# Eight kept weights' splits moved into the first part's down projection, half stores, and the tail as one written order

## The chip, the cores and the metric

One core of a Trainium2 chip runs the whole program. The metric is device time in microseconds of one launch; lower is better. Of the kernel before there are three timed runs and one profiled execution.

## The reference

One step of a two-layer backbone over 640 tokens (512 latent, 128 context) of width 1024. Layer 0 mixes by attention, layer 1 by a gated linear recurrence (LRU); each is followed by a gated feed-forward network of inner width 2816, and at the end stands one RMS norm. What matters for the change:

```python
def _swiglu(x, w_gu, w_down):
    gate, up = jnp.split(x @ w_gu, 2, axis=-1)
    return (jax.nn.silu(gate) * up) @ w_down

def _rms_norm(x, g):
    xf = x.astype(jnp.float32)
    y = xf * lax.rsqrt(jnp.mean(xf * xf, axis=-1, keepdims=True) + RMS_EPS)
    return (y * g.astype(jnp.float32)).astype(x.dtype)
...
    # each sub-layer: pre-norm, scale and shift from silu(cond) @ w_mod + b_mod, gated residual add
    y_prompt = _rms_norm(ctx, final_g)
    y_sample = _rms_norm(lat, final_g)
```

## The kernel before

Activations lie with the 1024 features on partitions in 8 tiles (`x[:, f, tokens]`), tokens along the free axis. Every product of fp32 data is made of three passes of matmuls: each operand is split into a rounded high half and the rest as low half, and `chunk` (L233) adds high x high (L240), high x low (L241) and low x high (L242) for each of the feature tiles into one PSUM tile (`mm` or `mx`). The split is a cast on ScalarE (ACT) and a subtraction on VectorE (DVE), `split`, L1443 and L1444. A weight that is used once is loaded through SyncE's queue as `raw` and split into `whi`/`wlo` or `whx`/`wlx` by `unit` (L174).

**Feed-forward of layer 0** (`ffn`, L838 to 878). The 22 inner tiles are done in three parts of 8, 7 and 7. In a part's gate and up stage, each inner tile j takes one gate and one up product; DVE multiplies with the norm's `r` and adds (`sg`, `up`), ACT applies SiLU, and the hidden tile is split into halves in `big`. Then the part's down projection follows: `project` (L567) runs over 8 output tiles f, each with a product over the part's tiles and a residual add to `x` (L562). The third part's down projection is also the entry to the next layer. In the trace: part one's gate and up stage 394 to 500 us, its down projection 500 to 556; part two 556 to 655 and 655 to 705; part three 705 to 805 and 805 to 860.

**Kept splits** (`keep`, L199 to 210, called in L872). 29 weights of the later layer, the recurrence's input and output products (16 `wi`, 8 `wlo`) and five tiles of the next feed-forward (`gu`), are split ahead of time, while PE is busy with layer 0's feed-forward, and the halves are put into DRAM; `unit` later loads both halves with no work on ACT and DVE. A keep is: load 512 KB into `mraw` (three buffers, shared with the modulations) through POOL's queue, cast on ACT (L207) and subtract on DVE (L208) into the two halves of one buffer `kw`, one store of 1 MB through POOL's queue (L210). It is issued behind the split of the last hidden tile (`self.mark`). Before, two are called in each step j of parts two and three, and three in the last step of each.

**Modulations** (`fill`, `mod_cols`, L271 to 281). The adaLN columns of later sub-layers are worked out in the background: a load of 512 KB into `mraw` through POOL's queue, and two DVE products with accumulation (`mprod`, L279), one for each of the two conditioning vectors. `done` and `ws` call `fill`.

**The tail** (`project_last`, L596 to 645). The last down projection is done in two token ranges, first 384 tokens for all 8 output tiles, then 256. In the second, each product p0 to p7 is followed by a residual add; ACT squares the sums, POOL adds squares up (L627). The final norm's statistics of a range: `root` (L483) takes the second moment by matmuls with ones (`at`, L488), then mean and root (`var`, a power on POOL or a square root with a correction step on ACT and DVE), `diag` (L504) puts the result on a diagonal (`dg`, L505), and `spread` (L507) brings it to all partitions by matmuls with ones (L509). Then DVE multiplies `x` by the column of `final_g` and the spread value (L613 for the first range, 8 of 384 columns; L640 for the second, 8 of 256), and SyncE stores pairs of tiles.

**What sets the order.** ACT, DVE, PE and POOL each run their instructions in program order. That order is set by a scheduler that interleaves the written steps, `issue_after` gives it edges, and a block under `in_order` keeps the order in which it is written.

Of the kernel before, what the change touches and what calls it, by code (L numbers as in the profile page):

```python
# [9 lines left out]
F32 = mybir.dt.float32  # L10
F32R = mybir.dt.float32r
AF = mybir.ActivationFunctionType
ALU = mybir.AluOpType
AX = mybir.AxisListType

P = 128
D = 1024
KT = D // P
# [17 lines left out]
ORDERED = (mybir.EngineType.PE, mybir.EngineType.DVE, mybir.EngineType.Activation)  # L36
C0 = 515
FG = (1, 1, 1)
MODS = ((0, 2), (0, 4), (0, 3), (0, 5), (1, 1), (1, 0), (1, 4), (1, 3), (1, 2), (1, 5))
NB = 2  # L40
KH = KT // 2
HT = NTOK // 2
# [11 lines left out]

COLS = ["ng00", "ng01", "ng10", "ng11", "cw0", "cw1", "cw2", "cw3", "cb",
        "ba0", "ba1", "bi0", "bi1", "lam0", "lam1", "h0", "h1", "bsh", "bsc", "fg"] + [f"bm{l}{j}" for l, j in MODS]
# [77 lines left out]
class _Step:  # L134
# [64 lines left out]
    def keep(self, todo, n):  # L199
        nc = self.nc  # L200
        for _ in range(min(n, len(todo))):
            name, f = key = todo.pop(0)
            raw = self.t([P, D], F32, "mraw", 3, self.sb).rearrange("p (k m) -> p k m", k=KT)
            nc.gpsimd.dma_start(raw, self.i[name][1, f] if name == "gu" else self.i[name][f])
            w = self.t([P, 2, KT, P], F32R, "kw", 1, self.sb)
            with self.tc.issue_after(self.mark[0]), self.tc.issue_after(self.mark[1]):
                nc.scalar.copy(w[:, 0], raw)  # L207
                nc.vector.tensor_tensor(w[:, 1], raw, w[:, 0].bitcast(F32), ALU.subtract)  # L208
            self.kept[key] = d = self.dram.tile([P, 2 * D], F32, tag=f"k{name}{f}", name=f"k{name}{f}")
            nc.gpsimd.dma_start(d, w.rearrange("p h k m -> p (h k m)").bitcast(F32))  # L210

    def two(self, src, x):
        nc = self.nc
# [257 lines left out]
    def square(self, k, t0, t1):  # L471
        nc = self.nc
        s = slice(t0, t1)
        if k == 0:
            nc.scalar.activation(self.ssq[:, s], self.x[:, k, s], AF.Square)
            return
        q = self.t([P, 384], F32, "sq", 2, self.sb)[:, :t1 - t0]
        self.sqr = nc.scalar.activation(q, self.x[:, k, s], AF.Square).ins
        if k < KT - 1 or self.whole:
            nc.vector.tensor_tensor(self.ssq[:, s], self.ssq[:, s], q, ALU.add)  # L480
        self.lastq[t0] = [q]
# [22 lines left out]
    def diag(self, dg, r, n):  # L504
        self.dg = self.nc.vector.tensor_tensor(dg, self.ident.unsqueeze(1).broadcast_to([P, n, P]), r.unsqueeze(2).broadcast_to([P, n, P]), ALU.mult).ins  # L505
# [90 lines left out]
    def project_last(self, w, hi, lo, gk):  # L596
        nc, tc = self.nc, self.tc
        G = self.need(self.gcols, gk)
        us = []
        for f in range(0, KT, 2):  # L600
            us += self.two(w[f:f + 2], f % 4)
        (a0, a1), (b0, b1) = CHL
        self.ssq = self.t([P, NTOK], F32, "ssq", 1, self.sb)
        for f, u in enumerate(us):
            self.residual(f, a0, a1, self.chunk(u, hi, lo, a0, a1), G, True)
        with tc.issue_after(self.sqr):
            nc.scalar.activation(self.t([P, 1], F32, "dum", 1), self.ones[:, 0:1], AF.Sqrt)
        mm = self.stat(a0, a1)
        r0 = self.r[0][:, 0:a1 - a0]

        def final(k):
            xs = self.x[:, k, a0:a1]
            nc.vector.scalar_tensor_tensor(xs, xs, self.col("fg", k), r0, ALU.mult, ALU.mult)  # L613

        def store(k, t0, t1):
            nc.sync.dma_start(self.o["y"][k * P - P:k * P + P, t0:t1].rearrange("(k p) t -> p k t", p=P), self.x[:, k - 1:k + 1, t0:t1])

        squares = []
        for f, u in enumerate(us):
            with tc.issue_after(mm) if f == KT - 1 else nullcontext():  # L620
                ps = self.chunk(u, hi, lo, b0, b1)
            last = self.residual(f, b0, b1, ps, G, False)
            xs = self.x[:, f, b0:b1]
            q = self.ssq[:, b0:b1] if f == 0 else self.t([P, HT], F32, "snap", 3, self.sb)[:, 0:b1 - b0]
            nc.scalar.activation(q, xs, AF.Square)
            if 0 < f < KT - 3:
                nc.gpsimd.tensor_tensor(self.ssq[:, b0:b1], self.ssq[:, b0:b1], q, ALU.add)  # L627
            squares.append(q)
            if f > 1:
                with tc.issue_after(last):  # L630
                    final(f - 2)
        self.lastq[b0] = squares[KT - 3:]
        self.stat(b0, b1, True)
        r1 = self.r[0][:, 0:b1 - b0]
        with tc.issue_after(self.dg):
            for k in range(KT - 2, KT):
                final(k)
        for k in range(KT):
            xs = self.x[:, k, b0:b1]
            nc.vector.scalar_tensor_tensor(xs, xs, self.col("fg", k), r1, ALU.mult, ALU.mult)  # L640
        for k in (1, 3):
            store(k, a0, a1)
        for t0, t1, ks in ((b0, b1, (1,)), (a0, a1, (5, 7)), (b0, b1, (3, 5, 7))):
            for k in ks:
                store(k, t0, t1)


    def qk(self, p, hi, lo, ap, acc=None):
        nc = self.nc
# [188 lines left out]
    def ffn(self, l, hi, lo, fp, last):  # L838
        nc = self.nc
        f0 = 0  # L840
        todo = [("wi", KT), ("wi", 0)] + [("wi", f + g) for f in range(1, KT) for g in (KT, 0)] + [("wlo", f) for f in range(KT)]
        todo += [("gu", c * NF + f) for f in range(PLAIN) for c in range(2)] + [("gu", PLAIN)]
        for ci, n in enumerate((8, 7, 7)):
            hhi = self.big()
            hlo = self.big()
            sg = {}

            def eg(j):
                def ev(t0, s, ps):
                    if t0:  # L850
                        sg[j] = self.t([P, NTOK], F32, "sg", 2, fp)
                    g = sg[j]
                    nc.vector.tensor_tensor(g[:, s], ps, self.rt[:, s], ALU.mult)
                    for c, a, b in _pieces(s.start, s.stop):
                        nc.scalar.activation(g[:, a:b], g[:, a:b], AF.Silu, bias=self.bias[:, c:c + 1])
                return ev

            def eu(j):
                def ev(t0, s, ps):
                    u = self.t([P, 320], F32, "up", 2, fp)  # L860
                    nc.vector.tensor_tensor(u, ps, self.rt[:, s], ALU.mult)
                    for c, a, b in _pieces(s.start, s.stop):
                        g = sg[j][:, a:b]
                        nc.vector.scalar_tensor_tensor(g, u[:, a - t0:b - t0], self.bias[:, c:c + 1], g, ALU.add, ALU.mult)
                    self.mark = self.split(hhi[:, j, s], hlo[:, j, s], sg[j][:, s])
                return ev
            for j in range(n):
                f = f0 + j
                self.ws(self.i["gu"][l, f], hi, lo, eg(j), FG[0] * (f > 0), CHB)
                self.ws(self.i["gu"][l, NF + f], hi, lo, eu(j), FG[1] * (f > 0), CHB)  # L870
                if ci:
                    self.keep(todo, 3 if j == n - 1 else 2)  # L872
            w = self.i["dn"][l, :, :, f0:f0 + n]
            if ci == 2:
                last(w, hhi, hlo, (l, 5))
            else:
                self.project(w, hhi, hlo, (l, 5), done=lambda f: self.fill(FG[2]))
            f0 += n


# [707 lines left out]
```

## Time and profile before

| | |
|---|---|
| median of 3 runs | 1515.62 us (1513.51 to 1517.41) |
| profiled execution, device time | 1514.37 us |
| its span | 1512.6 us |
| mean granted TensorE clock | 0.993 |
| PE / DVE / ACT / POOL busy | 98% / 71% / 47% / 17% |
| DMA, mean over the span | 163 GB/s |
| DMA, 556 to 655 us | 283 GB/s, 0.84 of the engines' time |

The profile's rows give busy time for each engine. A row of waits names the engine and line that waited, what released it, the total, the number of times and the longest. The chain of waits goes back from an end to what released each step, so a DMA in it is one that something stood still for. Rows of windows give busy time of each engine in a stretch, then the granted clock, the share of time that the 16 DMA engines were busy, and GB/s.

### The profile page before, as it was taken

What the parts mean: (1) busy time and instruction counts of PE and PEld (TensorE: products, weight loads), DVE (VectorE), ACT (ScalarE), POOL (GpSimd) and SP (SyncE); (2) the same over time, 40 slices, a digit from 0 to 9 for tenths busy, and PEclk for the clock granted to TensorE, in tenths of its full rate; (3) what the DMA queues carried; (4) which work ended last, traced back from release to release, by engine and by line L of the source; (5) the groups of instructions that cost most, each with busy time, mean ns of one, the idle gap of its engine ahead of it and who ended that gap; (6) DMA issues with size and microseconds to landing.
All of it is one profiled execution on the core that took longest, in us unless ns stands there. A gap on an engine that the chain in (4) does not pass through costs nothing.

```text
span 1512.6 us, 26116 instructions
## 1 busy us (share of the span) xinstructions
PE 1477.8 (98%) x10303; PEld 1432.5 (95%) x10303; DVE 1078.4 (71%) x2044; ACT 716.5 (47%) x1320; POOL 256.4 (17%) x315
## 2 busy tenths in 40 slices
PE   7999999999999999999999999999999999999997
PEld 4999999889999999999999988899999999999996
DVE  5788887869996337869787468885875675665646
ACT  5676766654333124322435378863644343424342
POOL 0212221100110001111111001122123323232211
PEclk9999999999999999999999999999999999999999
DMA  9554554445563228987898733246333131313111
GB/s 374 168 161 144 181 166 140 117 154 182 168 199 120 74 94 289 313 295 264 305 310 309 267 124 128 71 160 229 118 130 89 57 112 56 112 57 107 62 57 70
DMA packets 79530, 246.99 MB, mean 163 GB/s; under 512 B 8832, under 2 KB 22320, under 8 KB 75568
## 3 DMA queue, kind: packets, MB, share of 16 engines
q1 hardware_dynamic: 58416, 154.97, 31.3%
q0 software_dynamic: 20672, 90.20, 18.0%
q8 instruction: 81, 1.33, 0.4%
q14 instruction: 41, 0.34, 0.1%
q10 hardware_dynamic: 320, 0.16, 0.0%
HBM read 202.02 MB, written 39.34 MB: 160 GB/s over the span
## 4 chain that ended last, share of the span: by engine, by line
PE 79%; DMA 8%; DVE 6%; ACT 3%; issue 3%; POOL 1%; SPq 0%; POOLq 0%; DVEq 0%; ACTq 0%
PE mm L240 12%; PE mm L241 12%; PE mm L242 12%; PE mx L240 4%; PE mx L242 4%; PE mx L241 4%; PE mx L1132 3%; PE mx L1133 3%; PE mx L1134 3%; PE gp L1338 2%; DMA mraw<-in_wm 2%; PE op L826 2%; PE tp L743 2%; DMA kwi<-kw 1%; DMA kwlo<-kw 1%
## 5 line engine op out<-in xcount | busy, mean ns | idle before, releaser
L241 PE MATMUL mm<-big,whi 128*128 128x320 f32 (+2 forms) x1003 | 312.2, 311 | 4.0 <-DVE big L1444 4.0
L240 PE MATMUL mm<-big,whi 128*128 128x320 f32 (+2 forms) x1003 | 311.1, 313 | 1.8 <-ACT big L1443 1.0
L242 PE MATMUL mm<-big,wlo 128*128 128x320 f32 (+2 forms) x1003 | 311.8, 312 | 0.0
L279 DVE SCALAR_TENSOR_TENSOR mprod<-mraw,csb 128x1024 f32<-128x1024 f32 x160 | 195.9, 1225 | 9.3 <-DMA mraw<-in_wm 9.1
L241 PEld LDWEIGHTS mm<-big,whi 128*128 128x128 f32 x1003 | 189.8, 189 | 6.1 <-DVE big L1444 5.0
L240 PEld LDWEIGHTS mm<-big,whi 128*128 128x128 f32 x1003 | 189.2, 189 | 4.7 <-ACT big L1443 1.9
L242 PEld LDWEIGHTS mm<-big,wlo 128*128 128x128 f32 x1003 | 189.7, 189 | 1.1
L1443 ACT CAST whi<-raw 128x1024 fp32r<-128x1024 f32 (+2 forms) x103 | 105.7, 1027 | 150.3 <-PE mm L241 96.5
L1444 DVE TENSOR_TENSOR wlo<-raw,whi 128x1024 fp32r<-128x1024 f32 (+2 forms) x103 | 127.0, 1233 | 36.3 <-ACT whi L1443 36.0
L241 PE MATMUL mm<-big,whx 128*128 128x320 f32 (+3 forms) x450 | 140.0, 311 | 0.0
L242 PE MATMUL mm<-big,wlx 128*128 128x320 f32 (+3 forms) x450 | 140.0, 311 | 0.0
L240 PE MATMUL mm<-big,whx 128*128 128x320 f32 (+3 forms) x450 | 139.9, 311 | 0.0
L562 DVE SCALAR_TENSOR_TENSOR x<-mm,G,x 128x320 f32<-128x320 f32 (+3 forms) x207 | 83.5, 437 | 78.3 <-PE mm L242 70.4
L240 PE MATMUL mx<-big,whi 128*128 128x320 f32 (+2 forms) x325 | 101.7, 313 | 0.2 <-ACT whi L1443 0.2
L242 PE MATMUL mx<-big,wlo 128*128 128x320 f32 (+2 forms) x325 | 100.8, 310 | 0.0
L241 PE MATMUL mx<-big,whi 128*128 128x320 f32 (+2 forms) x325 | 100.6, 310 | 0.0
L275 POOL DMA_DIRECT2D mraw<-in_wm x80 | 43.2, 540 | 325.6 <-DVE mprod L279 211.3
L241 PEld LDWEIGHTS mm<-big,whx 128*128 128x128 f32 x450 | 85.6, 190 | 0.0
L240 PEld LDWEIGHTS mm<-big,whx 128*128 128x128 f32 x450 | 85.6, 190 | 0.0
L242 PEld LDWEIGHTS mm<-big,wlx 128*128 128x128 f32 x450 | 85.6, 190 | 0.0
L240 PE MATMUL mx<-big,whx 128*128 128x320 f32 (+3 forms) x222 | 69.1, 311 | 0.0
L242 PE MATMUL mx<-big,wlx 128*128 128x320 f32 (+3 forms) x222 | 69.0, 311 | 0.0
(370 smaller groups left out, 3813.3 us busy)
## 6 DMA issues: line engine op xcount, KB each, us to landing
raw<-in_gu SPq DMA_DIRECT2D x84, 512.0 KB, 3.6
mraw<-in_wm POOLq DMA_DIRECT2D x80, 512.0 KB, 4.3
kwi<-kw POOLq DMA_DIRECT2D x16, 1024.0 KB, 5.3
raw<-in_dn SPq DMA_DIRECT2D x24, 512.0 KB, 3.6
raw<-in_wqk SPq DMA_DIRECT2D x16, 512.0 KB, 4.0
sw<-in_wm SPq DMA_DIRECT2D x16, 512.0 KB, 10.2
mraw<-in_wi POOLq DMA_DIRECT2D x16, 512.0 KB, 5.2
kwlo<-kw POOLq DMA_DIRECT2D x8, 1024.0 KB, 5.2
```

The lines of the kernel that those rows point to most:

```text
L240: nc.tensor.matmul(ps, hi[:, k], xhi[:, k, s], start=(k == 0), stop=False)
L241: nc.tensor.matmul(ps, hi[:, k], xlo[:, k, s], start=False, stop=False)
L242: nc.tensor.matmul(ps, lo[:, k], xhi[:, k, s], start=False, stop=(k == nk - 1))
L275: nc.gpsimd.dma_start(w, self.i["wm"][l * 6 + j - 2, f])
L279: nc.vector.scalar_tensor_tensor(prod, w, 1.0, self.csb[:, s], ALU.mult, ALU.mult, accum_out=out[:, s, f:f + 1])
L562: last = self.nc.vector.scalar_tensor_tensor(xs, ps[:, a - t0:b - t0], G[:, s, f:f + 1], xs, ALU.mult, ALU.add).ins
L743: nc.tensor.transpose(tp[:, j * P:j * P + P], s[:, j * P:j * P + P], self.ident)
L1132: nc.tensor.matmul(ps, hi[:, k], xh[:, k], start=start and k == 0, stop=False, skip_group_check=not start)
L1133: nc.tensor.matmul(ps, hi[:, k], xl[:, k], start=False, stop=False, skip_group_check=not start)
L1134: nc.tensor.matmul(ps, lo[:, k], xh[:, k], start=False, stop=(k == KH - 1), skip_group_check=not start)
L1443: high = self.nc.scalar.copy(hi, v).ins
L1444: return high, self.nc.vector.tensor_tensor(lo, v, hi.bitcast(F32), ALU.subtract).ins
```

## The change

**Kept splits.** The buffer `kw` becomes two, `kwh` and `kwl`, and the 1 MB store two of 512 KB, both issued behind the subtraction in the program. Part one's down projection calls one keep behind each of its 8 output tiles. Part two calls two in each of the first six steps, part three in each of the first seven; 9 are left for it, so they go to steps 0 to 4. No keep is called at a part's last step.

**The tail.** Its steps stand in one written order (`TAIL`), kept on PE, DVE, ACT and POOL. The multiplication with `final_g` moves to ACT, on `x` itself (16 new activations with a column as scale: `gain`, 8 of 384 columns and 8 of 256), placed ahead of the finals. The finals become products with the spread value alone: four of two tiles with 384 columns, two of four tiles with 256, each with its store. POOL adds five squares instead of four, so the second moment is taken of three parts instead of four. The first range's moment (`m`) stands after p1 and its spread (`x`) after p3. Three matmuls with ones stand ahead of the last spread; nothing reads their result, which the spread overwrites.

```diff
+LATE = (0, 6, 7)
...
+TAIL = (
+    "p0 T r0 p1 m r1 q0 q1 t1 p2 d r2 q2 t2 p3 x r3 s0 s1 q3 t3 p4 F0 r4 F2 s2 q4 t4 p5 r5 F4 s3 q5 t5 p6 r6 s4 F6 q6 s5 s6 p7 r7 q7 s7 y67 ")
...
         for _ in range(min(n, len(todo))):
             name, f = key = todo.pop(0)
-            raw = self.t([P, D], F32, "mraw", 3, self.sb).rearrange("p (k m) -> p k m", k=KT)
-            nc.gpsimd.dma_start(raw, self.i[name][1, f] if name == "gu" else self.i[name][f])
-            w = self.t([P, 2, KT, P], F32R, "kw", 1, self.sb)
+            raw = self.t([P, D], F32, "mraw", 3, self.sb)
+            nc.gpsimd.dma_start(raw.rearrange("p (k m) -> p k m", k=KT), self.i[name][1, f] if name == "gu" else self.i[name][f])
+            self.kept[key] = d = self.dram.tile([P, 2 * D], F32, tag=f"k{name}{f}", name=f"k{name}{f}")
+            high, low = [self.t([P, D], F32R, n, 1, self.sb) for n in ("kwh", "kwl")]
             with self.tc.issue_after(self.mark[0]), self.tc.issue_after(self.mark[1]):
-                nc.scalar.copy(w[:, 0], raw)
-                nc.vector.tensor_tensor(w[:, 1], raw, w[:, 0].bitcast(F32), ALU.subtract)
-            self.kept[key] = d = self.dram.tile([P, 2 * D], F32, tag=f"k{name}{f}", name=f"k{name}{f}")
-            nc.gpsimd.dma_start(d, w.rearrange("p h k m -> p (h k m)").bitcast(F32))
+                nc.scalar.copy(high, raw)
+                nc.vector.tensor_tensor(low, raw, high.bitcast(F32), ALU.subtract)
+            for h, w in enumerate((high, low)):
+                nc.gpsimd.dma_start(d[:, h * D:h * D + D], w.bitcast(F32))
...
+        def gain(f, t0, t1):
+            nc.scalar.activation(x[:, f, t0:t1], x[:, f, t0:t1], AF.Copy, scale=self.col("fg", f))
...
-            nc.vector.scalar_tensor_tensor(xs, xs, self.col("fg", k), r0, ALU.mult, ALU.mult)
...
-        for k in range(KT):
-            xs = self.x[:, k, b0:b1]
-            nc.vector.scalar_tensor_tensor(xs, xs, self.col("fg", k), r1, ALU.mult, ALU.mult)
...
+        def final(k0, k1, t0, t1, r):
+            v = x[:, k0:k1, t0:t1]
+            nc.vector.tensor_tensor(v, v, r.unsqueeze(1).broadcast_to([P, k1 - k0, t1 - t0]), ALU.mult)
+            nc.sync.dma_start(self.o["y"][k0 * P:k1 * P, t0:t1].rearrange("(k p) t -> p k t", p=P), v)
+
+        def close(*ks):
+            self.lastq[b0] = [q[k] for k in ks]
+            s = self.stat_diag(self.stat_root(b0, b1, True))
+            ps = self.ps("mx")
+            for _ in range(3):
+                nc.tensor.matmul(ps[:, 0:b1 - b0], self.ones, self.ssq[:, b0:b1], start=True, stop=True)
+            self.spread(s[3], s[2], ps, b0)
+            for k in (0, KH):
+                final(k, k + KH, b0, b1, ps[:, 0:b1 - b0])
...
                 if ci:
-                    self.keep(todo, 3 if j == n - 1 else 2)
+                    self.keep(todo, 2 if j < LATE[ci] else 0)
...
-                self.project(w, hhi, hlo, (l, 5), done=lambda f: self.fill(FG[2]))
+                def between(f, n=1 - ci):
+                    self.fill(FG[2])
+                    self.keep(todo, n)
+                self.project(w, hhi, hlo, (l, 5), done=between)
```

What this does to the rows of the engines is shown at three places. First, DVE at part two's end, where the low half of the last hidden tile (`big<-sg`) is made. A row names the line, the operation, the written tile and the tiles read, and the size. Before:

```order
L279 SCALAR_TENSOR_TENSOR mprod_7338,B_1281_7085<-mraw_7334,csb_658 128x1024
L1444 TENSOR_TENSOR big_6367<-sg_7367,big_6366 128x320
L864 SCALAR_TENSOR_TENSOR sg_7367<-up_7468,bias_7435,sg_7367 128x320
L208 TENSOR_TENSOR kw_7323<-mraw_7321,kw_7323 128x1024
L279 SCALAR_TENSOR_TENSOR mprod_7406,B_1281_7085<-mraw_7404,csb_658 128x1024
L1444 TENSOR_TENSOR big_6367<-sg_7367,big_6366 128x320
L562 SCALAR_TENSOR_TENSOR x_4076<-mm_7500,G_792_3819,x_4076 128x192
```

Now, with the same two `big` rows as the last of part two:

```order
L1470 TENSOR_TENSOR big_6439<-sg_7463,big_6438 128x320
L884 TENSOR_TENSOR up_7564<-mx_7539,r_4651 128x320
L1470 TENSOR_TENSOR wlx_7749<-raw_7746,whx_7748 128x896
L284 SCALAR_TENSOR_TENSOR mprod_7434,B_1313_7173<-mraw_7430,csb_658 128x1024
L213 TENSOR_TENSOR kwl_7419<-mraw_7415,kwh_7418 128x1024
L887 SCALAR_TENSOR_TENSOR sg_7463<-up_7564,bias_7531,sg_7463 128x320
L284 SCALAR_TENSOR_TENSOR mprod_7502,B_1313_7173<-mraw_7500,csb_658 128x1024
L567 SCALAR_TENSOR_TENSOR x_4076<-mm_7575,G_792_3819,x_4076 128x192
L567 SCALAR_TENSOR_TENSOR x_4076<-mm_7575,G_792_3819,x_4076 128x128
L1470 TENSOR_TENSOR big_6439<-sg_7463,big_6438 128x320
```

The subtraction of a keep and a modulation's product still stand ahead of the last `big`, and the first residual add of the down projection (`x`) moved ahead of it. On PE, the last `big` is read 29 matmuls after the last product of the gate and up stage, where it was 49.

Second, DVE in the first part's down projection. Before:

```order
L562 SCALAR_TENSOR_TENSOR x_4076<-mx_5875,G_792_3819,x_4076 128x320
L1444 TENSOR_TENSOR wlo_6239<-raw_6236,whi_6238 128x1024
L562 SCALAR_TENSOR_TENSOR x_4076<-mm_5913,G_792_3819,x_4076 128x320
L562 SCALAR_TENSOR_TENSOR x_4076<-mx_5939,G_792_3819,x_4076 128x192
L562 SCALAR_TENSOR_TENSOR x_4076<-mx_5939,G_792_3819,x_4076 128x128
L1444 TENSOR_TENSOR wlx_6174<-raw_6171,whx_6173 128x1024
```

Now:

```order
L567 SCALAR_TENSOR_TENSOR x_4076<-mx_5875,G_792_3819,x_4076 128x320
L1470 TENSOR_TENSOR wlo_6293<-raw_6290,whi_6292 128x1024
L213 TENSOR_TENSOR kwl_5989<-mraw_5985,kwh_5988 128x1024
L284 SCALAR_TENSOR_TENSOR mprod_6129,B_1116_5978<-mraw_6127,csb_658 128x1024
L567 SCALAR_TENSOR_TENSOR x_4076<-mm_5922,G_792_3819,x_4076 128x320
L284 SCALAR_TENSOR_TENSOR mprod_6131,B_1116_5978<-mraw_6127,csb_658 128x1024
L567 SCALAR_TENSOR_TENSOR x_4076<-mx_5948,G_792_3819,x_4076 128x192
L567 SCALAR_TENSOR_TENSOR x_4076<-mx_5948,G_792_3819,x_4076 128x128
L213 TENSOR_TENSOR kwl_6063<-mraw_6059,kwh_6062 128x1024
```

Between the residual adds stand the kept splits, and products of the modulations, 12 in this stage where there were none; eight of them stood in the gate and up stage ahead of it.

Third, DVE at the program's end. Before:

```order
L499 SCALAR_TENSOR_TENSOR rs_16171<-rz_16173,ry_16172 128x2
L505 TENSOR_TENSOR dg_16179<-ident_63,rs_16171 128x256
L613 SCALAR_TENSOR_TENSOR x_11052<-x_11052,cols_61,mx_16011 128x384 x2
L640 SCALAR_TENSOR_TENSOR x_11052<-x_11052,cols_61,mx_16181 128x256 x8
L1584 UNCONDITIONAL_BRANCH
```

Now:

```order
L647 TENSOR_TENSOR x_11110<-x_11110,mx_16142 128x2x384
L567 SCALAR_TENSOR_TENSOR x_11110<-mm_16219,G_1483_8285,x_11110 128x128 x2
L496 TENSOR_SCALAR var_16244<-at_16237 128x2
L501 RECIPROCAL ry_16247<-ry_16247 128x2
L502 TENSOR_TENSOR rz_16248<-var_16244,ry_16247 128x2
L503 SCALAR_TENSOR_TENSOR rz_16248<-rz_16248,ry_16247 128x2
L504 SCALAR_TENSOR_TENSOR rs_16246<-rz_16248,ry_16247 128x2
L510 TENSOR_TENSOR dg_16254<-ident_63,rs_16246 128x256
L647 TENSOR_TENSOR x_11110<-x_11110,mx_16256 128x4x256 x2
```

The first range's last finals moved from behind `dg` to ahead of the last residual add, and eight finals became two.

More of the change, by code (lines that the diff above doesn't have):

```diff
@@ L603, in project_last @@
         self.ssq = self.t([P, NTOK], F32, "ssq", 1, self.sb)
+        x, q, bank, z = self.x, {}, {}, {}
+        def gain(f, t0, t1):
+            nc.scalar.activation(x[:, f, t0:t1], x[:, f, t0:t1], AF.Copy, scale=self.col("fg", f))
         for f, u in enumerate(us):
             self.residual(f, a0, a1, self.chunk(u, hi, lo, a0, a1), G, True)
-        with tc.issue_after(self.sqr):
-            nc.scalar.activation(self.t([P, 1], F32, "dum", 1), self.ones[:, 0:1], AF.Sqrt)
-        mm = self.stat(a0, a1)
@@ L609, in project_last @@
[L609 to L637, printed above, removed]
-        for k in range(KT):
-            xs = self.x[:, k, b0:b1]
[L640 to L645, printed above, removed]
+            gain(f, a0, a1)
@@ new lines, in load, with product, add, square @@
+        def load():
+            with tc.issue_after(self.sqr):
+                nc.scalar.activation(self.t([P, 1], F32, "dum", 1), self.ones[:, 0:1], AF.Sqrt)
+        def product(f):
+            bank[f] = self.chunk(us[f], hi, lo, b0, b1)
+        def add(f):
+            self.residual(f, b0, b1, bank[f], G, False)
+        def square(f):
+            q[f] = self.ssq[:, b0:b1] if f == 0 else self.t([P, HT], F32, "snap", 3, self.sb)[:, 0:b1 - b0]
+            nc.scalar.activation(q[f], x[:, f, b0:b1], AF.Square)
@@ new lines, in total, with moment, diag, spread @@
+        def total(f):
+            nc.gpsimd.tensor_tensor(self.ssq[:, b0:b1], self.ssq[:, b0:b1], q[f], ALU.add)
+        def moment():
+            z["a"] = self.stat_root(a0, a1)
+        def diag():
+            z["a"] = self.stat_diag(z["a"])
+        def spread():
+            self.stat_spread(z["a"])
+            z["a"] = self.r[0][:, 0:a1 - a0]
+        def final(k0, k1, t0, t1, r):
+            v = x[:, k0:k1, t0:t1]
+            nc.vector.tensor_tensor(v, v, r.unsqueeze(1).broadcast_to([P, k1 - k0, t1 - t0]), ALU.mult)
+            nc.sync.dma_start(self.o["y"][k0 * P:k1 * P, t0:t1].rearrange("(k p) t -> p k t", p=P), v)
@@ new lines, in close, with scale, finals @@
+        def close(*ks):
[7 more added lines that the diff above has]
+                final(k, k + KH, b0, b1, ps[:, 0:b1 - b0])
+        def scale(f):
+            gain(f, b0, b1)
+        def finals(k):
+            final(k, k + 2, a0, a1, z["a"])
@@ L648, in qk @@
+        steps = dict(T=load, p=product, r=add, q=square, t=total, s=scale, m=moment, d=diag, x=spread, F=finals, y=close)
+        with self.in_order(ORDERED + (mybir.EngineType.Pool,)):
+            for step in TAIL.split():
+                steps[step[0]](*map(int, step[1:]))
     def qk(self, p, hi, lo, ap, acc=None):
```

## Prediction

> **What bounds the kernel now.** I read the page's first rows, then PE's waits, then the chain of waits around the waits found, then busy time by stage.
>
> ```profile
> span 1512.6 us, 26116 instructions
> PE 1477.8 (98%) x10303; PEld 1432.5 (95%) x10303; DVE 1078.4 (71%) x2044; ACT 716.5 (47%) x1320; POOL 256.4 (17%) x315
> ```
>
> TensorE (PE) is busy 1477.8 us of 1512.6. The change removes no matmul of the products and adds three small ones, so all it can win lies in the 35 us in which PE stands, and in stretches where PE is busy at a lower clock. PE's waits, as total us, times, longest:
>
> ```profile
> PE mm L241 <- DVE big L1444: 4.0, 2, 2.1
> PE mx L509 <- DVE dg L505: 3.0, 2, 1.8
> PE mm L240 <- ACT big L1443: 1.0, 2, 0.6
> ```
>
> In each row one wait lies in a place that the change touches: 2.1 us at the end of the second feed-forward part (652.96 to 655.06), both waits of the tail's spread (1.2 and 1.8), and 0.6 at the third part's end (before 804.86). The other waits of these rows lie at 291 us and elsewhere ahead of the change. The chain of waits ahead of the first one:
>
> ```profile
> 643.54 7.26 DMA mraw<-in_wm
> ...
> 650.82 0.04 DVE mprod L279
> ...
> 652.05 0.40 DVE up L861
> 652.46 1.00 DVE wlx L1444
> ...
> 654.60 0.42 DVE big L1444
> ...
> 655.06 0.42 PE mm L241
> ```
>
> VectorE (DVE) takes its queue in order. A modulation product (`mprod`) waited for a load that took 7.26 us, and the low half of the last hidden tile (`big`) stood behind it. The wait has a second price, in the clock (us, PE, PEld, DVE, ACT, POOL, granted clock, DMA share, GB/s):
>
> ```profile
> 640.00:652.90 12.90, 12.90 (x87) 12.58 (x86) 9.03 (x17) 4.57 (x8) 2.65 (x5) 1.00 0.92 324
> 652.90:655.10 2.20, 0.10 (x2) 0.04 (x1) 2.20 (x5) 1.05 (x1) 0.20 (x1) 1.00 0.83 274
> 655.10:658.00 2.90, 2.90 (x14) 2.90 (x14) 2.90 (x5) 0.46 (x1) 1.38 (x3) 0.64 0.74 243
> 658.00:661.00 3.00, 3.00 (x18) 3.00 (x18) 1.88 (x5) 0.14 (x1) 0.53 (x1) 0.78 1.04 367
> ```
>
> After the gap the granted clock is 0.64 for 2.9 us and 0.78 for 3.0: 2.9 x 0.36 + 3.0 x 0.22 = 1.7 us of lost matmul time. [...]
>
> **The kept splits.** Each keep is a load (512 KB), a cast on ACT, a subtraction on DVE and, before, one store of both halves from one buffer. So a keep can't begin before the last one's store has landed:
>
> ```profile
> 564.77 5.29 DMA kwi<-kw
> 570.15 1.06 ACT kw L207
> 571.23 1.24 DVE kw L208
> ...
> 572.75 5.28 DMA kwi<-kw
> ```
>
> From store to store that is 572.75 - 564.77 = 8.0 us, and two are wanted in each step of 14.2 us (99 us for 7 steps), so 7.1 each. The chain falls behind until its work stands around the part's end. In the changed kernel the halves have a buffer and a store each. The nearest row for a 512 KB transfer is the page's median from issue to landing of the loads:
>
> ```profile
> mraw<-in_wm POOLq DMA_DIRECT2D x80, 512.0 KB, 4.3
> ```
>
> The high half's cycle is a cast and a store, 1.06 + 0.3 + 4.3 = 5.7 us; the low half's 1.24 + 0.3 + 4.3 = 5.8. From below the store is half of the 5.28 of 1 MB (a cycle of 4.2), from above the 7.26 us of the load above (8.8, worse than before). I take 5.8, since 4.3 is the median of 80 transfers of this size: under the 7.1 that are wanted. [...]
>
> Where the keeps move to (us, PE, PEld, DVE, ACT, POOL, clock, DMA share, GB/s; first down projection, part two's gate and up; then, past its down projection, part three's gate and up):
>
> ```profile
> 500.00:556.00 56.00, 56.00 (x381) 56.00 (x380) 19.38 (x31) 9.80 (x12) 0.00 (x0) 1.00 0.25 76
> 556.00:655.00 99.00, 96.96 (x657) 96.58 (x655) 72.98 (x123) 39.42 (x69) 16.00 (x31) 1.00 0.84 283
> 705.00:805.00 100.00, 99.41 (x674) 99.15 (x673) 81.24 (x138) 40.44 (x74) 17.48 (x33) 1.00 0.87 300
> ```
>
> *First down projection.* It gets 8 keeps, and by the written order 12 `mprod` more that stood in the stages around it. The price of one `mprod`; that of a keep's subtraction and cast (1.24, 1.06) stands in the chain above:
>
> ```profile
> L279 DVE SCALAR_TENSOR_TENSOR mprod<-mraw,csb 128x1024 f32<-128x1024 f32 x160 | 195.9, 1225 | 9.3 <-DMA mraw<-in_wm 9.1
> ```
>
> DVE: 19.4 + 8 x 1.24 + 12 x 1.23 = 44 of 56 us. ACT: 9.8 + 8 x 1.06 = 18. Both have room. DMA: 76 GB/s x 56 us = 4.3 MB, 8 x (0.52 + 1.05) = 12.6 MB of keeps, 6 loads of 0.52 = 3.1 MB: 20 MB, of which about 1.5 (the last stores) may land later; 18.5 / 56 = 330 GB/s. The rows show 283 to 300 GB/s over 50 to 100 us and 324 over 13 us. So this stage is at the DMA's limit. At 310 (between these) it ends 4 us late. What covers it: PE goes on while residual adds are late by up to the free PSUM tiles, three of five, some 3.5 us each (8 x 3 matmuls of 0.148 us, 12.9 us for 87 in the row above): 10 us. Cost taken: 0; without the cover, 4 us and a dip of 1.7.
>
> *Part two.* 12 keeps, the same number that stand ahead of the last `big` on DVE before, and 19 `mprod` (17 before). None is issued at the last step any more, but one of step 5 still stands ahead of the last `big` in DVE's rows, with three `mprod` and now two residual adds. Whether the wait goes depends on the pace: 12 x 5.8 = 70 us against 12 x 8.0 = 96 of the stage's 99, so the last keep is done 20 us or more before the end as far as the chain is concerned. In bytes: 12 x 1.57 + 9.5 x 0.52 + 7.3 for gate and up + 1.8 for the next down weights less 1.5 that may land later = 31.4 MB, 101 us at 310 GB/s and 97 at 324. By the chain the wait goes, by the bytes it is open. PE needs the last `big` 29 matmuls (4.3 us) after its last gate and up chunk now, 49 (7.3 us) before, so that lateness is forgiven less. I take the wait as gone, since before the loads queued behind 1 MB stores that came in bursts and now 8 keeps less lie in what follows: **-2.1 us, and -1.7 us of clock**. Bounds: 0 (the wait stays) and +4 (it is longer by the shorter cover, 7.3 - 4.3 = 3 us, and more).
>
> *Part three's end.* The cause there:
>
> ```profile
> 797.12 6.07 DMA kgu<-kw
> ...
> 803.29 1.05 ACT kw L207
> 804.34 0.48 ACT big L1443 x2
> ...
> 804.86 0.57 PE mm L240 x2
> ```
>
> A kept cast waited 6.07 us for a store on ACT's queue, with the last hidden cast behind it. In the changed order no keep is left in the third part's last steps (9 remain, done by step 4): **-0.6 us**, clock unchanged since the row showed no dip there. What was the last down projection's DMA (4 keeps) shrinks too; nothing waited for it.
>
> **The tail.** The chain there:
>
> ```profile
> 1491.22 1.23 PE at L488 x12
> ...
> 1492.79 0.12 PE mm L240
> ...
> 1493.80 0.48 DVE dg L505
> ...
> 1494.32 0.94 PE mx L509 x6
> ...
> 1502.15 1.07 PE at L488 x8
> ...
> 1504.46 0.42 DVE dg L505
> 1504.89 1.05 DVE x L613 x2
> ...
> 1506.33 2.74 DVE x L640 x7
> ```
>
> The first moment's sum (`at`) stands two products earlier now, after p1, with the spread still after p3. A product is 12 matmuls of 0.12 us, 1.4. Before, p3 ended at about 1493.2, after the four matmuls from the row of 1492.79 on; p1 then ends at 1493.2 - 1.23 - 2 x 1.4 = 1489.2, `at` at 1490.4, and `dg` 1.83 us later (before from 1491.22 + 1.23 = 1492.45 to 1494.28) at 1492.2, ahead of p3's end: the first spread's 1.2 us goes. The 16 new ACT gains (525 ns for 384 columns, 412 for 256) lie between squares:
>
> ```profile
> L478 ACT ACTIVATE sq<-x 128x384 f32<-128x384 f32 x7 | 3.6, 525 | 3.1 <-DVE ssq L480 2.2 <-DVE x L562 0.7
> L625 ACT ACTIVATE snap<-x 128x256 f32<-128x256 f32 x7 | 2.6, 412 | 9.9 <-DVE x L562 9.8 <-POOL ssq L627 0.2
> ```
>
> Six of the first pass's eight come ahead of its last square: 6 x 0.525 = 3.15 us, as much as the 3.1 us that ACT stood idle between the squares of that row. So the last square comes a few tenths later, and p1's end at 1489.2 leaves it that. The second moment has three parts for four: two groups of eight matmuls at 1.07 before, so 2.1 / 4 = 0.5 us less. The finals behind it (the second row is the window that holds the last stores):
>
> ```profile
> L640 DVE SCALAR_TENSOR_TENSOR x<-x,cols,mx 128x256 f32<-128x256 f32 x8 | 3.2, 477 | 0.0
> 1507.00:1511.00 4.00, 0.00 (x0) 0.00 (x0) 2.07 (x6) 0.00 (x0) 0.00 (x0) 0.50 0.99 346
> ```
>
> From 1505.94 (1504.89 + 1.05) eight products start every 0.4 us, 3.2 us; now two of 1024 elements at the 1.24 of the kept split's subtraction of that size, 2.5 us, -0.7; the last 384-column pair (1.05) no longer stands behind `dg`, -0.2. On DVE: 1.2 + 0.5 + 0.7 + 0.2 = 2.6, the last final ends at 1506.5 instead of 1509.1. The stores bind, though: DMA runs at 346 GB/s and 0.99 share from 1507 to 1511. Now 1.05 MB start only when the first big final is done (1505.3, plus 1 us to the first byte): 1506.35 + 3.05 = 1509.4, where the last byte landed at 1511.2. **-1.8 us**. The three warming matmuls (an estimate from the first spread's six of 128 columns in 0.94 us: six passes of 256 columns, 0.9 to 1.9 us) lie in PE's idle time after the second moment (1503.2 to 1504.9): 0; if they aren't done when `dg` is, up to +0.5. Bounds of the tail: -2.6 (DVE binds) and -0.6 (the first moment is late, its 1.2 us stay).
>
> **Sum.** 1514.37 (span 1512.6 and 1.8 around it) - 2.1 - 1.7 - 0.6 - 1.8 = 1508.2. The profiled execution is 1.2 under the median of 1515.62, so 1509.4.
>
> **Rivals.** (a) *The wait at part two's end stays.* For it: the kept split and the `mprod` that stand ahead of the last `big`, 31 MB in 99 us, loads of 7.26 us. Against: the chain has 20 us of room. Only -0.6 and -1.8 are left: 1515.6 - 2.4 = 1513.2. Chance 0.27. (b) *Slower: the DMA can't carry the moved bytes.* If the stores as halves hold the rate at 300 GB/s or less, the first down projection's 20 MB take 67 us for 56 (11 late) and part two's 33 MB take 110 for 99 (11 late). DVE and ACT stand in order behind kept splits; covers of 10 and 4 leave 1 + 7 us on PE, and two dips of 1.7: 1509.4 + 11.4 = 1520.8. It decides from a landing of a 512 KB store over about 7 us. For it: the 330 GB/s worked out above. Against: 324 and 346 GB/s in the rows. Chance 0.13, half of it under 1520. (c) *The tail gives little:* the gains put the last square past p1, `at` waits, -0.6 in place of -1.8: 1510.6; with PE's wait and cold clock ahead of the last spread, 1511.5. Chance 0.12. (d) That the change doesn't do what it says is no case here: the rows of the order above show each move.
>
> **The numbers.** Forecast 0.48, (a) 0.27, (b) 0.13, (c) 0.12. A measurement here tells 0.3%, 4.5 us, from no change: faster is under 1511.1, slower over 1520.2. Faster: 0.42 of the forecast's 0.48, half of (c), a little of (a): 0.50. Slower: half of (b) and a little: 0.08. Same: 0.42. The range goes from 1506.5 (tail at -2.6, and 2 us more from keeps out of the down projections) to 1516.5 (beyond (a), into (b)).
>
> **What would show it.** Right: no PE wait on `big` in the kernel's part two or three ends, clock 1.00 there, kept splits under 7 us apart, DMA about 320 GB/s in the first down projection with PE at 56 us, one wait on `dg` instead of two, the last stores 1.8 us earlier. Wrong: PE under 100% in the first down projection, PE still waiting on `big` after part two, or PE waiting for `at` or its clock at 0.5 in the products of the tail.

## The result and the profile after

The changed kernel takes 1509.39 us (median of 5 runs, 1508.27 to 1510.54), the kernel before 1516.17 beside it (5 runs, 1513.51 to 1518.08): a ratio of 0.996, 95% interval 0.9945 to 0.9974, so 3.9 to 8.3 us less. One run of `moved_only` below, 2067.63 us, was in the slow state and is left out of its ratio and median. The profiled execution has a span of 1507.3 us, 5.3 less than before.

The page's first rows of the changed kernel, and its PE waits (total, times, longest):

```profile
span 1507.3 us, 26208 instructions
PE 1477.6 (98%) x10305; PEld 1430.9 (95%) x10305; DVE 1079.3 (72%) x2034; ACT 722.2 (48%) x1336; POOL 272.6 (18%) x345
```
```profile
PE mm L246 <- DVE big L1470: 2.2, 2, 1.9
PE mm L245 <- ACT big L1469: 1.4, 3, 0.8
```

PE is as busy as before. No wait for the spread's diagonal is left among the large ones. Of the two rows shown, 1.9 us is the old wait at 292 us; 0.8 + 0.3 = 1.1 us stand at part two's end, where 2.1 stood. Part three's end has none. The same windows as before (us, PE, PEld, DVE, ACT, POOL, clock, DMA share, GB/s):

```profile
500.00:556.00 56.00, 56.00 (x381) 56.00 (x380) 41.94 (x67) 15.67 (x18) 14.33 (x27) 1.00 0.94 337
556.00:655.00 99.00, 97.89 (x662) 97.36 (x661) 78.97 (x133) 38.99 (x70) 24.32 (x46) 1.00 0.88 302
...
705.00:805.00 100.00, 100.00 (x680) 100.00 (x679) 74.82 (x128) 40.42 (x75) 17.54 (x33) 1.00 0.70 246
```

The first down projection moves 337 GB/s with DMA at 0.94, DVE works 42 us of 56, and PE stands nowhere in it. Part three's DMA fell from 300 to 246 GB/s. What is left at part two's end, in the chain of waits:

```profile
641.71 7.21 DMA mraw<-in_wm
...
648.95 0.04 DVE mprod L284
...
650.10 0.08 DVE mprod L284
650.18 0.41 DVE big L1470
650.60 0.04 issue
650.64 0.41 PE mm L246
```

It is the chain of before in kind: a load of 7.2 us, the product that waits for it, and the last `big` behind it. Only its lateness shrank. The tail's chain:

```profile
1475.07 0.62 PE mm L245 x2
```
```profile
1489.72 0.67 PE mx L514 x6
...
1497.28 0.62 PE at L493 x4
...
1499.13 0.44 DVE dg L510
1499.61 0.73 PE mx L514 x4
1500.36 1.22 DVE x L647
1501.59 1.13 DVEq L1610
```

The first spread (L514 x6) follows a product with no wait. From the first product of this stage (1475.07) to the span's end it is 32.2 us, before 1512.6 - 1478.52 = 34.1, with 1478.52 from this row of the kernel before:

```profile
1478.52 0.62 PE mm L240 x2
```

Where no stretch at half clock falls into it, this distance is 34.1 to 34.3 us in every profile of the old tail and 32.2 to 32.4 in every one of the new with two last stores, and the experiments below are read by it.

### The profile page after: what moved, and what is told of

It reads as the page before. It is cut to its first block, busy times and chain, and to the rows that moved or that the text cites. A ratio compares the mean times of both kernels' runs of the same rounds, so it can differ in the third digit from the quotient of the medians.

```text
span 1507.3 us, 26208 instructions
## 1 busy us (share of the span) xinstructions
PE 1477.6 (98%) x10305; PEld 1430.9 (95%) x10305; DVE 1079.3 (72%) x2034; ACT 722.2 (48%) x1336; POOL 272.6 (18%) x345
## 4 chain that ended last, share of the span: by engine, by line
PE 82%; DVE 6%; DMA 5%; issue 3%; ACT 3%; POOL 1%; SPq 0%; DVEq 0%; POOLq 0%; ACTq 0%
PE mm L246 12%; PE mm L247 12%; PE mm L245 12%; PE mx L245 4%; PE mx L247 4%; PE mx L246 4%; PE mx L1158 3%; PE mx L1159 3%; PE mx L1160 3%; PE gp L1364 2%; DMA mraw<-in_wm 2%; PE op L849 2%; PE tp L766 2%; PE mc L1158 1%; PE mc L1160 1%
## 6 DMA issues: line engine op xcount, KB each, us to landing
sw<-in_wm SPq DMA_DIRECT2D x16, 512.0 KB, 10.2
```

## The experiments

Because the timed runs of one kernel scatter by several us, each run is read by its place in the trace as well. For each profiled execution: PE's waits at part two's end and at part three's end, the time at half clock behind them, and the time from the tail's first product to the end; waits of under 0.2 us are left out. A star marks an old tail with 3.4 us at half clock behind its first spread's wait.

| kernel | part two | part three | half clock | tail | profiled execution / median, us | timed ratio to before (95%) |
|---|---|---|---|---|---|---|
| before | 2.10 | 0.59 | 3.4 | 34.1 | 1514.37 / 1516.17 | |
| before, again | 0.80 | 1.37 | 0 | 35.7* | 1515.01 | |
| tail_only | 1.37 | 1.37 | 0 | 32.3 | 1512.57 / 1510.76 | 0.9963 (0.995 to 0.9977) |
| keep_only | 0.94 | 0 | 0 | 34.3 | 1511.53 / 1512.83 | 0.9982 (0.9968 to 0.9997) |
| halves_only | 0 | 3.18 | 3.4 | 35.9* | 1519.02 / 1511.53 | 0.9979 (0.9962 to 0.9995) |
| moved_only | 2.88 | 0 | 0 | 34.1 | 1509.19 / 1516.17 | 1.0004 (0.9987 to 1.0022) |
| no_move | 0 | 2.46 | 3.4 | 32.3 | 1515.67 / 1511.53 | 0.997 (0.9953 to 0.9986) |
| changed | 1.11 | 0 | 0 | 32.2 | 1509.39 / 1509.39 | 0.996 (0.9945 to 0.9974) |
| changed, again | 0 | 0 | 0 | 32.3 | 1513.07 | |
| late57 | 0 | 0 | 0 | 32.2 | 1509.83 / 1509.15 | 0.9962 (0.9947 to 0.9977) |
| no_warm | 0.52 | 0 | 0 | 32.4 | 1509.73 / 1511.5 | 0.9973 (0.9954 to 0.9991) |
| four_stores | 0.96 | 0 | 0 | 31.6 | 1507.93 / 1508.38 | 0.9961 (0.9943 to 0.9979) |
| late57_four | 0 | 0 | 0 | 31.6 | 1507.85 / 1507.85 | 0.9946 (0.9927 to 0.9965) |
| twice_moved | 7.45 | 0 | 10.2 | 32.2 | 1520.82 / 1513.98 | 1.0004 (0.9987 to 1.0021) |

A row of waits tells what happened in one execution, and not always in a typical one: in halves_only, no_move and twice_moved the profiled execution is the slowest of 12, 10 and 10, in moved_only the fastest of 11. What an edit is worth is read from the ratio, each to runs of the kernel before beside it. The changed kernel's second profile has no wait at the part ends and still takes 3.7 us more than its first, so several us of an execution lie outside the places in this table.

The theory is the sum of the prediction: waits at two part ends plus a tail. The rivals are that only the tail gives the gain, that place or pace alone counts for the keeps, and that the moved bytes stop PE.

**One half each.** `keep_only` is the changed kernel with `project_last` of before; `tail_only` is the kernel before with `project_last` and `TAIL` of the changed one.

> The kept splits as in the changed kernel, the tail as before. If the terms add up as forecast, the feed-forward of layer 0 is 3.1 to 4.4 us shorter than before and the tail is the old one: a ratio of 0.997 to 0.998, with both waits on the spread's diagonal (1.2 and 1.8 us) back. The rival, that nearly all of the gain is the tail's, gives 0 to -1 us here.

> The tail as in the changed kernel, the kept splits as before. By the forecast's term the span's end comes 1.8 us earlier (bounds 0.6 to 2.6): ratio 0.999, PE's wait of 2.1 us at part two's end and the low clock behind it stay. The rival, that the tail's gain is held by the stores anyway, gives 0. A gain over 3 us would say that the kept splits did nothing.

Both halves gain against the kernel before. In the traces the waits at the part ends are 0.94 us in keep_only and 2.74 in tail_only; the tail is 34.3 and 32.3 us. So 1.8 to 2 us come from each. The timed ratio of tail_only, 3.5 to 7.6 us less, is more than its trace shows in the tail; that of keep_only, 0.5 to 4.8 less, agrees. A gain of over 3 us was named as a sign that the kept splits did nothing, and by the timed runs tail_only is as fast as the whole change (0.9963 and 0.996). So what the kept splits give rests on keep_only, whose interval is only just clear of no change, and on the waits in the traces; what they add to the new tail isn't shown by the timed runs.

**Half stores or the new places.** `halves_only` has the changed `keep` and everything else as before. `moved_only` is keep_only with the `keep` of before:

```diff
-            high, low = [self.t([P, D], F32R, n, 1, self.sb) for n in ("kwh", "kwl")]
...
-            for h, w in enumerate((high, low)):
-                nc.gpsimd.dma_start(d[:, h * D:h * D + D], w.bitcast(F32))
+            w = self.t([P, 2, KT, P], F32R, "kw", 1, self.sb)
...
+            nc.gpsimd.dma_start(d, w.rearrange("p h k m -> p (h k m)").bitcast(F32))
```

> Half stores from two buffers, but two keeps in each step of parts two and three and three at the last step as before, nothing in the first down projection, the tail as before. If the pace of the store chain (8.0 us against 5.8) made the wait at part two's end, it is gone or under 1 us here and the time falls by 2 to 4 us. If what is called at a part's end made it, the wait of about 2 us and the clock's loss of 1.7 stay or grow, since three keeps and their loads still come in the last step, and the time is that of before within 1 us.

> The keeps in the places of the changed kernel, but with one buffer and one store of 1 MB as before, the tail as before. By the pace: 8 keeps of 8.0 us take 64 us for the first down projection's 56, so the chain runs over into part two, 12 more take 96 of 99, and the wait at part two's end stays at 2 us or grows (0 to +4 us against before). If the place alone counts, the waits at both parts' ends go and it is 3 to 4 us under before, like the changed kernel's feed-forward.

In its profile each takes away one of the two waits and worsens the other. With one store of 1 MB in the new places, part two's chain has a store in it:

```profile
641.39 6.10 DMA kwlo<-kw
647.52 0.04 ACTq L211
...
648.54 0.46 ACT big L1450
649.01 0.04 issue
649.05 0.41 PE mm L244
```

PE waits 2.9 us. With half stores in the old places, part two has no wait, but part three, with three keeps in its last step, has 3.2 us. The window of that wait and the one behind it (same columns):

```profile
798.80:802.00 3.20, 0.02 (x1) 0.00 (x0) 2.33 (x5) 0.46 (x1) 1.06 (x2) 1.00 0.75 299
802.00:807.00 5.00, 4.88 (x22) 4.66 (x23) 4.03 (x7) 2.36 (x4) 0.53 (x1) 0.68 0.86 297
```

In these two executions neither reading holds alone. The timed runs speak for the half stores: halves_only and keep_only, which have them, are 4.6 and 3.3 us under moved_only by their medians, and moved_only, with the new places alone, is no faster than before (1.0004), though the intervals just overlap. That the new places add anything to half stores isn't shown here (0.9979 without, 0.9982 with them).

**Is the move into the first down projection needed?** `no_move` is the changed kernel with this edit:

```diff
-                    self.keep(todo, 2 if j < LATE[ci] else 0)
+                    self.keep(todo, 2 if ci == 1 else (3, 3, 3, 2, 2, 2, 0)[j])
...
-                def between(f, n=1 - ci):
+                def between(f, n=0):
```

> The changed kernel's half stores and tail, but nothing kept in the first down projection: two keeps in each step of part two and 3, 3, 3, 2, 2, 2, 0 in part three. If half stores and an empty last step of part three do the work, both parts' ends have waits under 1.1 us together, as the changed kernel, and the move into the first down projection is worth nothing (ratio 0.995 to 0.997). If the move is needed for room, the waits are 2 us or more, and the time is 1 to 4 us over the changed kernel's.

In the profile it is needed. Part two is free of waits with 14 keeps, but part three, with 15, waits 2.5 us though no keep is called in its last step:

```profile
792.43 7.03 DMA kgu<-kwl
799.55 1.23 DVE kwl L213
800.77 0.60 DVE sg L887 x2
801.40 0.47 ACT big L1469
801.91 0.41 PE mx L245
```

A kept split of an earlier step waits 7.0 us for its buffer's store, and the last hidden tile stands behind it on DVE. The timed runs leave it open against the changed kernel, whose interval overlaps (0.997 and 0.996). Timed in the same round, late57_four below, which has the move and 10 and 11 keeps in parts two and three, is 3.7 us faster by the medians, and of that its four stores explain 0.7 in the traces (32.3 to 31.6). So the move is likely worth some us there, but how much isn't settled.

**The limit of the move.** `twice_moved` calls two keeps behind each output tile (`n=2 - 2 * ci`).

> The changed kernel with two keeps behind each of the first down projection's 8 output tiles instead of one: 16 there, 12 in part two, 1 in part three. 16 keeps are 25 MB and with the rest over 32 MB in 56 us, 570 GB/s, which no row shows (337 at most): the stage falls about 40 us behind, past the 10 us that free PSUM tiles cover. By the rival of the prediction that moved bytes stop PE, PE waits 10 to 30 us and the clock falls: +10 to +40 us. If the loads only shift into part two with the order giving way, under 3 us.

The first down projection still doesn't stop. Of its 16 kept subtractions only 9 start before 556 us; the work slips into part two, and PE stands 7.45 us at its end, then 10.2 us at half clock (10.2 / 2 = 5.1 us more):

```profile
500.00:556.00 56.00, 56.00 (x381) 56.00 (x380) 31.69 (x49) 15.91 (x17) 13.24 (x25) 1.00 0.86 308
556.00:655.00 99.00, 95.72 (x649) 95.45 (x647) 74.52 (x122) 39.30 (x71) 24.94 (x47) 1.00 0.89 319
655.00:668.00 13.00, 8.83 (x44) 8.83 (x45) 10.40 (x19) 3.41 (x6) 4.08 (x8) 0.64 0.85 286
```

Its chain there has a load of 9.25 us. So 12.5 us are lost in this execution, the slowest of the ten, and one part later than expected. By the timed runs the loss against the changed kernel is about 6.7 us (1.0004 against 0.996), less than the 10 to 40 expected for a PE that stops and more than the 3 expected for work that only shifts.

**One keep fewer at part two's end.** `late57` is the changed kernel with `LATE = (0, 5, 7)`.

> The changed kernel with two keeps in each of the first five steps of part two instead of six (10 instead of 12), 11 left for part three. If the keeps still close to part two's end make the 1.1 us of waits that are left there, these go: -1 us against the changed kernel, ratio to before 0.995, with no new wait at part three's end (11 keeps end at step 5). If the modulations' loads make them (7.2 us from issue to landing), 0.3 to 1.1 us of wait stay and the time is the same.

PE has no wait in either stage of the profiled execution:

```profile
556.00:655.00 99.00, 99.00 (x673) 99.00 (x673) 84.21 (x145) 37.89 (x68) 22.86 (x43) 1.00 0.86 296
705.00:805.00 100.00, 100.00 (x680) 100.00 (x679) 73.93 (x124) 42.39 (x77) 19.67 (x37) 1.00 0.78 271
```

The changed kernel, profiled again, has none either. So how much late57 gains isn't settled by these profiles, and the timed ratios are alike.

**The tail.** `no_warm` leaves out the loop of three matmuls. `four_stores` ends with

```diff
-            for k in (0, KH):
-                final(k, k + KH, b0, b1, ps[:, 0:b1 - b0])
+            for k in range(0, KT, 2):
+                final(k, k + 2, b0, b1, ps[:, 0:b1 - b0])
```

> The changed kernel without the three matmuls ahead of the last spread. If they cost nothing and keep the clock up, PE stands about 1.7 us before the last spread and the spread takes up to 0.7 us more at half clock: 0 to +0.7 us. If they delay the spread, -0.3 us.

> The changed kernel with the second range's finals in four products of two tiles, each with a store of 256 KB, instead of two of four tiles with 512 KB. If the stores set the end, the first bytes leave 0.6 us earlier and the end comes 0.3 to 0.6 us earlier, though DVE ends no earlier. If DVE sets the end, 0 or +0.2 us.

Without the three matmuls the old wait on the diagonal is back in the records of no_warm:

```profile
PE mx L514 <- DVE dg L510: 1.8, 1, 1.8
```

It costs 0.2 us only in the trace (32.4 for 32.2); the timed ratio is higher than the changed kernel's (0.9973 and 0.996), with overlapping intervals. Four stores give 0.6 in the trace: the stores, not DVE, set the end. The timed runs don't resolve 0.6 us (0.9961). In the changed kernel's last window that holds them (same columns) DMA is full and DVE idle:

```profile
1503.00:1505.60 2.60, 0.00 (x0) 0.00 (x0) 0.00 (x0) 0.00 (x0) 0.00 (x0) 0.61 0.99 342
```

**Both, and repeats.** `late57_four` has both edits.

> The changed kernel with 10 keeps in part two and 11 in part three, and with four stores of 256 KB at the end. If the two gains seen apart add up (1.1 us of waits at part two's end, 0.7 us from the last products to the span's end), the profile has no PE wait of over 0.2 us between 560 and 860 us, 31.9 us from the tail's first product to the end, and the time is 1.8 us under the changed kernel's: ratio to before 0.9945 to 0.9965. If one hides the other, 0.7 to 1.1 us.

> The kernel before, profiled a second time. If the half clock behind the wait at part two's end follows from the wait, the profile shows the wait of 2.1 us and 3.4 us at half clock behind it again. [...]

> The changed kernel, profiled a second time. Waits at part two's end of 0.5 to 1.2 us, none at part three's end, 32.6 us from the tail's first product to the end. If the stretch at half clock near 380 us, which the profile of before has and that of the changed kernel has not, comes by chance, it may be here.

late57_four has no PE wait in the parts and the tail at 31.6 us: 1507.85 us, 0.9946 (0.9927 to 0.9965) of before. It beats the kernel before clearly; that it beats the changed one is likely by the traces, but the two intervals overlap. In the second profile of before, the wait at part two's end was 0.8 us, and behind it the clock stayed at 1.00; behind the first spread's 1.2 us, where the first profile shows nothing, it fell:

```profile
652.90:654.20 1.30, 0.50 (x3) 0.24 (x3) 1.30 (x4) 0.75 (x1) 0.40 (x1) 1.00 0.75 118
654.20:658.00 3.80, 3.80 (x27) 3.80 (x27) 3.80 (x8) 0.46 (x1) 1.19 (x3) 1.00 0.86 295
1493.20:1494.60 1.40, 1.31 (x9) 1.32 (x10) 0.37 (x2) 0.00 (x0) 0.00 (x0) 0.83 0.04 12
1494.60:1498.60 4.00, 4.00 (x25) 4.00 (x24) 1.41 (x4) 1.03 (x3) 0.66 (x1) 0.63 0.27 98
```

The stretch near 380 us isn't in the second profile of the changed kernel either; it is in six of the fourteen profiles, of before and changed code alike.

## Why the prediction was right, and where a step of it was off

The time forecast, 1509.4, is the time measured. That it agrees so closely is luck: the interval of the gain is 4.4 us wide, and the sum came right partly by errors that cancel. Of the signs named for a right prediction, the first down projection's DMA (337 GB/s) with PE at 56 us, the single wait on `dg` (0.3 us) and the end of the tail 1.9 us earlier came. Two did not: PE still waits 1.1 us on `big` at part two's end, and the kept splits are 8.0 us apart, not under 7.

- **The tail, -1.8: right.** Measured -1.9 (34.1 to 32.2), and that the stores bind is shown by four_stores. The first spread's wait went as worked out. The three matmuls with ones cost nothing, as taken: 32.2 us with them, 32.4 in no_warm.
- **Part three's end, -0.6: right in kind, and too small in size.** The wait was 0.6 in one profile of the old keep code and 1.4 in two (before again, tail_only); on average 1.1. It is gone in all seven profiles with the changed places (five) or those of late57 (two).
- **Part two's wait, -2.1: mis-sized.** It was 2.1, 0.8 and 1.4 in the three profiles of the old keep code, and with the changed keeps it is 1.1, 0, 0.9, 0.5 and 1.0. The means are 1.4 and 0.7. So about -0.7 in place of -2.1: rival (a) had half of the truth, and the 2.1 was the largest of three samples. Both ends together, old keeps wait 2.5 us on average, the changed 0.7: -1.8 for a forecast of -2.7.
- **The pace of the chain, 5.8 us for a keep: wrong.** The step took 4.3 us for a 512 KB store. In the changed kernel such stores land in 5.7 and 5.9 us in the median between 500 and 655 us:

```profile
kwi<-kwl POOLq DMA_DIRECT2D x15, 512.0 KB, 5.7
kwi<-kwh POOLq DMA_DIRECT2D x14, 512.0 KB, 5.9
```

  Half the bytes took no less time than 1 MB before (5.3). Two reasons are possible: in 10 of 18 keeps the second half's store is issued within 2.4 us of the first, so that both are under way together, and the DMA is busier (0.88 for 0.84 in part two). No run tells them apart. The 12 kept subtractions of part two start from 565.3 to 653.0 us, 8.0 each, so the 20 us of room ahead of the part's end weren't there. In the old places the first 12 start 8.2 to 8.4 us apart with one store (the two profiles of before) and 7.4 with half stores (halves_only); in the new ones 8.3 with one store (moved_only) and 8.0 with half stores. So half stores buy 0.3 to 0.9 us of pace, not 2.2: halving cost nothing here and gained a little. That the wait at part two's end shrank goes with the half stores: it is 0 in halves_only and no_move, without the move and with keeps called in the part's last step, and 2.9 us in moved_only, with the new places. These are single profiles, but the timed runs of halves_only and moved_only point the same way.
- **The clock, -1.7: not a price that each wait has.** It is real where it falls (before, halves_only, no_move, twice_moved), but waits of 0.8 to 1.4 us at part two's or three's end had none behind them, and neither had one of 2.9 us (moved_only), while 1.2 us in the tail had one in two of five old tails. What decides between them no run shows. A wait removed takes away the chance of 1.7 us, not the 1.7.
- **First down projection, 0: right.** 330 GB/s were worked out, 337 measured, and PE stayed at 56.0 of 56. Rival (b) fell at one keep for each tile; twice_moved shows its price, but at the next part's end. There the kept work slips behind the stage (31.7 us of DVE in it for 41.9) and PE never stands in it; whether free PSUM tiles cover it, as the prediction has it, isn't shown.

By place this explains -1.8 and -1.9, and with the chances of half clock (one in three profiles of old keeps, two in five of old tails, 1.7 us each) -0.6 and -0.7: 5.0 us, an estimate from few profiles, inside the measured 3.9 to 8.3. Why the timed ratio of tail_only lies lower than its trace explains stays open; stretches at half clock near 294, 318 and 380 us, in code that the change doesn't touch, come and go between executions at 1.7 us each.

## What to carry to other kernels

A stall seen in one profiled execution is a sample: profile the same kernel twice before its size goes into a sum, above all for a wait that hangs on DMA and for low clock behind it (2.1 and 0.8 us at part two's end in the two profiles of before, half clock behind the first alone). Where a DMA-fed chain runs close to its limit, take the landing time from the stretch where it will run, not from the median of all transfers of its size (5.7 and 5.9 us here, where 4.3, the median of 80 loads, was taken). Spread background work over the stages whose DMA has room (a share of 0.25 in the first down projection before, 0.94 after, PE at 56.0 of 56 us in both), so that its chain ends ahead of the last step before a dependent stage, since a late buffer held what stood behind it on DVE (in no_move a kept split behind a store of 7.0 us, and the last hidden tile behind that split). That nothing is called in the last step wasn't enough (2.5 us in no_move). And set a profiled execution's time beside the median of the runs before its waits are taken for the kernel's.

## What the runs showed of the hardware that was not expected

Stretches at half clock inside the products were all of one length but for one: 3.41 us each in the traces of before (from 294.10, 317.99, 379.43 and 655.91 us on) and of the changed kernel (from 295.25 and 319.14 us on), 3.4 in the other profiles, and once 10.24 us (twice_moved). Whether one followed a wait wasn't set by the wait's length alone: 2.88 us (moved_only) had none, 2.10 us (before) had one, 1.17 us (before again, halves_only) had one, 1.17 us (before, keep_only, moved_only) had none. The wait at part two's end and what came behind it, in before and in moved_only (same columns):

```profile
652.50:655.91 3.41, 1.31 (x10) 1.05 (x9) 3.41 (x6) 1.46 (x2) 0.53 (x1) 1.00 0.76 260
655.91:659.32 3.41, 3.41 (x15) 3.41 (x14) 3.41 (x7) 0.05 (x1) 1.06 (x2) 0.50 0.84 295
```
```profile
646.10:649.10 3.00, 0.12 (x2) 0.05 (x1) 1.19 (x3) 1.51 (x3) 0.00 (x0) 1.00 1.00 398
649.10:655.00 5.90, 5.90 (x40) 5.90 (x41) 5.87 (x11) 2.05 (x3) 1.58 (x3) 1.00 0.74 246
```

In before PE stands 2.1 us, and 0.85 us after it goes on, 3.41 us at 0.50 begin. In moved_only it stands 2.88 us, and the 5.9 us behind them are at 1.00. In halves_only the half clock behind the wait of 3.2 us begins at about 803.8 us (0.96 from 802 to 804 us, 0.50 from 804 to 806), 1.8 us after the wait's row ends.

Half clock came without a wait too. Near 380 us PE doesn't stand: in before it is busy for all of the 3.43 us ahead of the stretch (376 to 379.43 us), partly with the second moment of a norm, in matmuls of one column:

```profile
L488 PE MATMUL at<-ones,sq 128*128 128x1 f32 x12 | 1.5, 250 | 0.0
```

The stretch that follows in before comes in six of the fourteen profiles and not in the other eight. What decides, there and behind the waits, isn't shown: no run was made to test it.
